# Wide matmuls on high and low parts in two of seven products, and attention's values as a set of products

## The chip, the cores and the metric

The kernel runs on one core of a Trainium2 chip. The metric is device microseconds for one execution, from runs on the chip. A kernel is run several times, and the median is compared.

TensorE (PE in the profile) multiplies: it holds a stationary tile of up to 128x128 numbers, streams a moving tile of up to 512 columns past it, and adds the result to a bank of PSUM, of which there are eight with 512 columns of float32 each. VectorE (DVE), ScalarE (ACT) and GpSimd (POOL) work on tiles in SBUF. SyncE (SP), ACT and POOL also issue DMA transfers. Every engine takes its own instructions in order.

## The reference, cut to what matters

One block on 512 tokens of width 1024, all in float32: a feed-forward stage, a mixer and a second feed-forward stage, each added to x, and a last norm.

```python
def swiglu(x, w_gu, w_down):
    g, u = jnp.split(x @ w_gu, 2, axis=-1)
    return (jax.nn.silu(g) * u) @ w_down

def hybrid_mixer(h, w_in, conv_w, gate_w_up, gate_b, gla_norm_g, w_out_conv, w_out_gla, w_o):
    z = h @ w_in
    cb, cc, cu, q, k, v, g_lr, r, ga, gb = jnp.split(z, SPLIT_POINTS, axis=-1)
    y_conv = (cb * causal_short_conv(cc * cu, conv_w)) @ w_out_conv
    log_a = jax.nn.log_sigmoid((g_lr @ gate_w_up + gate_b).astype(jnp.float32)) / GATE_TAU
    o = gla_chunked(q, k, v, log_a)            # 4 heads, chunks of 64 tokens
    ...                                        # o: norm by head, times gla_norm_g
    y_gla = (o * jax.nn.silu(r)) @ w_out_gla
    merged = jax.nn.sigmoid(ga) * y_conv + jax.nn.sigmoid(gb) * y_gla
    return merged @ w_o

def reference(x, ...):
    x = x + 0.5 * swiglu(rmsnorm(x, norm_ffn1_g), ffn1_w_gu, ffn1_w_down)
    x = x + hybrid_mixer(rmsnorm(x, norm_mix_g), w_in, ...)
    x = x + 0.5 * swiglu(rmsnorm(x, norm_ffn2_g), ffn2_w_gu, ffn2_w_down)
    return rmsnorm(x, final_norm_g)
```

The hidden width of the feed-forward stages is 2816; the mixer's `w_in` has 8208 columns, of which 1024 make attention's values `v`.

## The kernel before, in words

**Numbers in two parts.** TensorE multiplies float32 numbers rounded to a shorter form (`F32R`). Each operand is therefore split: ACT casts it to a high part `h`, DVE subtracts that from the number for a low part `l` (weights: `wh` and `wl`, L309 and L310). A product is three matmuls: high by high, high by low, low by high.

**Sets of seven products.** Most matrices are multiplied two by two blocks at a time with seven products instead of eight, named `m1`, `p2`, `q6`, `p5`, `q7`, `p4`, `p3`. Their operands are sums of blocks. On the weight side, `s3` is a sum by DVE (L296), and three more sums are accumulating DMA transfers of POOL (`f<-f`, L287). On x's side `Operands.sum` makes the sums and `Operands.make` splits them once for all sets of a stage. A set (`Set`, L478) keeps three banks: `a`, `b` and `c`. Each product is 24 matmuls of 256 columns (L501). After `m1`, `q6` and `q7`, ACT copies bank `b` to SBUF (L506), and `done` adds such copies to the banks `a` and `c` with DVE. `order` interleaves neighbouring sets: `m1` of the next one comes ahead of `p4` of this one, then `p2` of the next, `p3` of this, and `q6`, `p5`, `q7` of the next.

**The stages.** A feed-forward stage (`ffn`) makes four plain pairs of gate and up columns (`mm_group`, `mm_single`, 512-column matmuls), then nine sets of two pairs each (`up_set`), then the down product (`down_product`): two sets with 512-column matmuls whose moving operand is the weights (`run_wide`, order of products `SEQ`), and the last six k-tiles plainly. The mixer (`mixer`) makes queries and keys of heads 0 and 1 with `mm_group`, half of `v` with `mm_wide` (L378 to L380), queries and keys of heads 2 and 3 with `mm_single`, the second half of `v`, then twelve sets listed in `MSETS`, the eight columns of `w_out_conv`, two sets of `w_out_gla` (`gla_done`), and `w_o`. Attention's steps for a head (`gates`, `decays`, `scale`, `scores`, `state`, `output`, `squares`) are put between these matmuls by hand, from the dictionary `hooks`. While `normed` overwrites x in place, x itself waits in DRAM (`xs`) and comes back with `reload` (L1453) for the sum in `evac`.

**Weights.** `Weights` works ahead: `take` hands out a split weight tile and has the tiles two steps ahead cast and split; `fetch` asks for plain tiles up to `early` steps ahead, and `phase` plans the loads of a set six steps ahead of its `m1`. Raw tiles share ten buffers (`f`), split ones three each (`wh`, `wl`).

**Order and memory.** The framework takes the instructions in the program's order as priorities and settles each engine's order and each tile's buffer when it builds the program. PSUM has one pool `ps` of six banks (`MM`) for the whole kernel and one of two (`AUX`).

Of the kernel before, what the change touches and what calls it, by code (L numbers as in the profile page):

```python
# [56 lines left out]


def wide(mat, kt, col):
    return [(mat, k0, 2, (col,), 512) for k0 in range(0, kt, 2)]  # L60
# [61 lines left out]
MSETS = [("ga", 0), ("gb", 0), ("conv", 0), ("ga", 1), ("conv", 1), ("gb", 1), ("conv", 2),  # L122
# [7 lines left out]
def wide_sets(mat):  # L130

    for w in range(WIDE):
        subs = []
        for u in range(2):
            subs.append(len(PLAN))
            PLAN.extend((mat, 8 * w + 4 * j + 2 * u, 2, (512 * c,), 512)
                        for c in range(2) for j in range(2))
        for p in SEQ:
            STEPS.extend((n, p) for n in subs)


def ffn_plan(up, down, plain, slow):
# [6 lines left out]
    wide_sets(down)  # L149
# [4 lines left out]
def mixer_plan():  # L154
    units(group("w_in", KD, (QO, KO, QO + P, KO + P)))
    units(wide("w_in", KD, VO))
# [3 lines left out]
    units(wide("w_in", KD, VO + 512))  # L160
# [23 lines left out]
def block_kernel(ctx: ExitStack, tc: tile.TileContext, xT, vecs, gf, gup, wgl, wts, out):  # L184
# [6 lines left out]
    ps = ctx.enter_context(tc.tile_pool(name="ps", bufs=6, space=bass.MemoryType.PSUM))  # L191
# [21 lines left out]
    def MM():  # L213
        cnt[0] += 1
        return ps.tile([P, S], F32, tag="mm", name=f"mm{cnt[0]}")
# [27 lines left out]
    class Weights:  # L243
# [13 lines left out]
        def phase(self, early, first=6):  # L257
# [12 lines left out]
        def fetch(self, at):  # L270

            for n, p in STEPS[at : min(at + self.early, self.end)]:
                if p is None and n not in self.raw:
                    self.raw[n] = self.dma(n)
                elif p is not None and STEPS[at][1] is None:
# [75 lines left out]
    def mm_group(mat, kt, cols, ah, al, extra=None, slow=False):  # L351
        o = [MM() for _ in cols]
        n = len(cols)
        for u in group(mat, kt, cols, slow):
            h, l = W.take(u)
            for i in range(u[2]):
# [6 lines left out]
                if extra is not None:  # L363
                    extra(k)
        return o

    def mm_wide(mat, kt, col, ah, al, extra=None):
        o = [MM() for _ in range(NTB)]
        for u in wide(mat, kt, col):
            h, l = W.take(u)  # L370
            for i in range(u[2]):
                k = u[1] + i
                wh = h[:, i * 512 : (i + 1) * 512]
                wl = l[:, i * 512 : (i + 1) * 512]
                for t in range(NTB):
                    a = ah[k][:, t * P : (t + 1) * P]
                    b = al[k][:, t * P : (t + 1) * P]
                    nc.tensor.matmul(o[t], a, wh, start=k == 0, stop=False)  # L378
                    nc.tensor.matmul(o[t], a, wl, start=False, stop=False)
                    nc.tensor.matmul(o[t], b, wh, start=False, stop=k == kt - 1)  # L380
# [97 lines left out]
    class Set:  # L478
# [8 lines left out]
        def run(self, p):  # L487
# [5 lines left out]
            bh, bl = self.group.get(p)  # L493
# [1038 lines left out]
```

## Time and profile before

| | |
|---|---|
| median of 3 runs | 1191.23 us (1188.14 to 1192.05) |
| the profiled execution | 1192.07 us, its span 1190.4 us |
| mean granted TensorE clock | 0.997 |
| busy share of the span | PE 99%, weight loads 91%, DVE 74%, ACT 53%, POOL 10% |
| matmuls | 7818, of them 5376 with 256 columns in sets |
| DMA | 197.10 MB, 166 GB/s |

The rows of the groups read: line, engine, operation, out<-in by the program's names, stationary and moving shape, count; then busy time in us, mean ns of one; then idle time before them and what ended it. The rows of a timeline and of the chain read: start in us, duration, what. The rows of a window read: its stretch and length, busy us of PE, PEld (weight loads), DVE, ACT and POOL with the counts, then granted clock, the share of the DMA engines and GB/s. The rows of waits read: who waited, for whom, us in total, times, longest.

### The profile page before, as it was taken

What the parts mean: (1) busy time and instruction counts of PE and PEld (TensorE: products, weight loads), DVE (VectorE), ACT (ScalarE), POOL (GpSimd) and SP (SyncE); (2) the same over time, 40 slices, a digit from 0 to 9 for tenths busy, and PEclk for the clock granted to TensorE, in tenths of its full rate; (3) what the DMA queues carried; (4) which work ended last, traced back from release to release, by engine and by line L of the source; (5) the groups of instructions that cost most, each with busy time, mean ns of one, the idle gap of its engine ahead of it and who ended that gap; (6) DMA issues with size and microseconds to landing.
All of it is one profiled execution on the core that took longest, in us unless ns stands there. A gap on an engine that the chain in (4) does not pass through costs nothing. (4 is left out here: it accounts for less than half of the span.)

```text
span 1190.4 us, 19195 instructions
## 1 busy us (share of the span) xinstructions
PE 1177.9 (99%) x7818; PEld 1085.6 (91%) x7818; DVE 878.5 (74%) x1044; ACT 625.5 (53%) x777; POOL 116.3 (10%) x155
## 2 busy tenths in 40 slices
PE   9999999999999999999999999999999999999997
PEld 8899999988788889999999998988889999998876
DVE  7976666897578765868688688676598666679955
ACT  6564454675245465646454566543345454566543
POOL 0011111101010001011111100200001101101100
PEclk9999999999999999999999999999999999999999
DMA  9477777678532325766877766741537777757721
GB/s 349 85 207 187 183 181 191 153 196 209 195 110 85 89 71 149 205 179 178 206 218 176 189 181 200 208 128 54 186 72 210 173 193 176 182 156 192 170 81 71
DMA packets 61224, 197.10 MB, mean 166 GB/s; under 512 B 6768, under 2 KB 13040, under 8 KB 61136
## 3 DMA queue, kind: packets, MB, share of 16 engines
q0 software_dynamic: 18560, 67.12, 30.7%
q1 hardware_dynamic: 37936, 124.27, 29.8%
q10 hardware_dynamic: 4640, 4.49, 1.2%
q8 instruction: 61, 1.00, 0.3%
q14 instruction: 27, 0.22, 0.1%
HBM read 124.55 MB, written 8.39 MB: 112 GB/s over the span
## 5 line engine op out<-in xcount | busy, mean ns | idle before, releaser
L501 PE MATMUL mm<-op,wh 128*128 128x256 f32 x3584 | 649.6, 284 | 2.8 <-ACT tp L506 2.8
L309 ACT CAST wh<-f 128x1024 fp32r<-128x1024 f32 (+1 forms) x335 | 350.1, 1046 | 439.4 <-PE mm L501 227.2
L501 PEld LDWEIGHTS mm<-op,wh 128*128 128x128 f32 x3584 | 560.2, 192 | 4.0 <-ACT tp L506 3.0
L310 DVE TENSOR_TENSOR wl<-f,wh 128x1024 fp32r<-128x1024 f32 (+1 forms) x335 | 406.9, 1217 | 182.2 <-ACT wh L309 176.5
L501 PE MATMUL mm<-op,wl 128*128 128x256 f32 x1792 | 508.1, 284 | 0.1
L501 PEld LDWEIGHTS mm<-op,wl 128*128 128x128 f32 x1792 | 344.0, 192 | 0.6 <-DVE wl L310 0.5
L287 POOL DMA_DIRECT2D f<-f x120 | 103.5, 866 | 922.1 <-DVE wl L310 477.1
L337 PE MATMUL mm<-op,wh 128*128 128x512 f32 x192 | 75.1, 391 | 0.0
L339 PE MATMUL mm<-op,wl 128*128 128x512 f32 x192 | 74.9, 390 | 0.0
L338 PE MATMUL mm<-op,wh 128*128 128x512 f32 x192 | 74.7, 389 | 0.0
L361 PE MATMUL mm<-op,wh 128*128 128x512 f32 x256 | 63.8, 391 | 0.2 <-DVE op L412 0.2
L791 PE MATMUL mm<-wl,op 128*128 128x512 f32 x160 | 62.6, 391 | 0.8 <-DVE wl L310 0.8
L789 PE MATMUL mm<-wh,op 128*128 128x512 f32 x160 | 62.3, 389 | 0.0
L793 PE MATMUL mm<-wh,op 128*128 128x512 f32 x160 | 62.2, 389 | 0.0
L361 PEld LDWEIGHTS mm<-op,wh 128*128 128x128 f32 x256 | 47.8, 188 | 10.6 <-issue 0.4
L506 ACT COPY tp<-mm 128x512 f32<-128x512 f32 x96 | 55.7, 580 | 1.9 <-DVE tp L1299 1.0
L296 DVE TENSOR_TENSOR f<-f,f 128x1024 f32<-128x1024 f32 x40 | 48.8, 1221 | 0.7
L339 PEld LDWEIGHTS mm<-op,wl 128*128 128x128 f32 x192 | 36.0, 188 | 7.5
L337 PEld LDWEIGHTS mm<-op,wh 128*128 128x128 f32 x192 | 36.1, 188 | 7.4
L338 PEld LDWEIGHTS mm<-op,wh 128*128 128x128 f32 x192 | 36.1, 188 | 7.4
L791 PEld LDWEIGHTS mm<-wl,op 128*128 128x128 f32 x160 | 30.0, 188 | 7.8 <-DVE wl L310 1.9
L789 PEld LDWEIGHTS mm<-wh,op 128*128 128x128 f32 x160 | 30.0, 188 | 6.3
(282 smaller groups left out, 1328.8 us busy)
## 6 DMA issues: line engine op xcount, KB each, us to landing
f<-wts SPq DMA_DIRECT2D x219, 512.0 KB, 4.4
f<-f POOLq DMA_DIRECT2D x120, 512.0 KB, 5.0
X<-xT SPq DMA_DIRECT2D x8, 256.0 KB, 5.2
xs<-X POOLq DMA_DIRECT2D x8, 256.0 KB, 2.3
ga<-tp ACTq DMA_DIRECT2D x8, 256.0 KB, 3.0
gb<-tp ACTq DMA_DIRECT2D x8, 256.0 KB, 4.9
tp<-ga SPq DMA_DIRECT2D x8, 256.0 KB, 6.0
X<-xs POOLq DMA_DIRECT2D x8, 256.0 KB, 7.5
```

The costliest lines, as they stand in the source:

```text
L287: nc.gpsimd.dma_start(out_, a, accum_op=ALU.add)
L309: self.cast = nc.scalar.copy(h[:, :w], raw[:, :w]).ins
L310: nc.vector.tensor_tensor(out=l[:, :w], in0=raw[:, :w], in1=h[:, :w].bitcast(F32), op=ALU.subtract)
L337: nc.tensor.matmul(o, wh, ah, start=first, stop=False)
L338: nc.tensor.matmul(o, wh, al, start=False, stop=False)
L339: nc.tensor.matmul(o, wl, ah, start=False, stop=last)
L361: nc.tensor.matmul(o[c], w[:, s : s + P], a[k], start=k == 0 and j == 0, stop=k == kt - 1 and j == 2)
L501: nc.tensor.matmul(to, ww[:, s], aa[:, t], start=fresh and k == 0 and e == 0 and j == 0, stop=k == 3 and j == 2, skip_group_check=True)
L506: nc.scalar.copy(v, o)
L789: nc.tensor.matmul(o[t], bh[:, s], wh, start=fresh and k == 0, stop=False, skip_group_check=True)
L791: nc.tensor.matmul(o[t], bh[:, s], wl, start=False, stop=False, skip_group_check=True)
L793: nc.tensor.matmul(o[t], bl[:, s], wh, start=False, stop=k == 3, skip_group_check=True)
```

## The change

1. **Up sets.** `up_set` uses a new `PairSet`. In products `p5` and `p3`, x's operand lies with its high and low part side by side (`Both`), and the high weights are multiplied by both at once: 8 matmuls of 512 columns, then 8 of 256 for the low weights by the high part. Bank `c` becomes a pair of banks (`MM2`); its halves are added by two DVE operations.
2. **First sums.** In all sets but a stage's first (`forked`), ACT copies the bank of `m1` into a new bank `a`, and `p2` adds to it; DVE's addition of `m1` goes. `q7`'s copy in up sets gets its sign on ACT.
3. **PSUM.** The pool of six banks is opened anew for each stage (`banks`); in the up sets it is two single banks and two pairs, and bank `a` comes from the other two.
4. **Values.** `v` is a set of seven products with 512-column matmuls (`natural_set`, taken from `run_wide`) behind the four single products. Since it is multiplied from the normed x, keys are scaled by the row once instead of by its square. Gates, decays and scaling of head 0 go between the single products, and all later steps of attention move to later sets; two sets of `MSETS` change places.
5. **x.** Each k-tile of x is read back by SP into a tile of its own during `w_out_conv`; POOL's eight reads go.
6. **Weight loads.** Inside sets, `fetch` looks three steps ahead instead of `early`; a set behind wide ones loads eight steps ahead.

```diff
-MSETS = [("ga", 0), ("gb", 0), ("conv", 0), ("ga", 1), ("conv", 1), ("gb", 1), ("conv", 2),
+MSETS = [("ga", 0), ("gb", 0), ("ga", 1), ("conv", 0), ("gb", 1), ("conv", 1), ("conv", 2),
...
 def mixer_plan():
     units(group("w_in", KD, (QO, KO, QO + P, KO + P)))
-    units(wide("w_in", KD, VO))
     for h in (2, 3):
         units(single("w_in", KD, QO + h * P))
         units(single("w_in", KD, KO + h * P))
-    units(wide("w_in", KD, VO + 512))
+    wide_sets("w_in", 1, VO)
...
+    def banks():
+        cnt[0] += 1
+        stack = ExitStack()
+        pools["ps"] = stack.enter_context(tc.tile_pool(
+            name=f"ps{cnt[0]}", bufs=6, space=bass.MemoryType.PSUM, reuse_waits="tile"))
+        return stack
+
+    def MM(bufs=6):
+        cnt[0] += 1
+        return pools["ps"].tile([P, S], F32, tag="mm", name=f"mm{cnt[0]}", bufs=bufs)
+
+    def MM2():
+        cnt[0] += 1
+        return pools["ps"].tile([P, 2, S], F32, tag="mm2", name=f"mm2_{cnt[0]}", bufs=2)
...
                 if p == "m1":
-                    self.loads.setdefault(max(lo, i - first), []).append(n)
+                    after = STEPS[i - 1][1] is not None and PLAN[STEPS[i - 1][0]][4] > HW
+                    wait = PLAN[n][4] == HW and after
+                    self.loads.setdefault(max(lo, i - (8 if wait else first)), []).append(n)
...
-            for n, p in STEPS[at : min(at + self.early, self.end)]:
+            inside = at < self.end and STEPS[at][1] is not None
+            for n, p in STEPS[at : min(at + (3 if inside else self.early), self.end)]:
...
+    class PairSet:
+        DUP = ("p5", "p3")
...
+            if fresh:
+                self.bank[n] = {"a": AUX, "b": lambda: MM(2), "c": MM2}[n]()
...
+            if p in self.DUP:
+                for k in range(4):
+                    for e in range(2):
+                        nc.tensor.matmul(o[:, e], h[:, k * HW + e * P : k * HW + (e + 1) * P],
+                                         x_.both(k), start=fresh and k == 0, stop=False,
+                                         skip_group_check=True)
+                for k in range(4):
+                    for e in range(2):
+                        nc.tensor.matmul(o[:, e, :HW], l[:, k * HW + e * P : k * HW + (e + 1) * P],
+                                         x_.high(k), start=False, stop=k == 3,
+                                         skip_group_check=True)
+            else:
...
+            if p == "m1" and self.forked:
+                self.bank["a"] = AUX()
+                nc.scalar.copy(self.bank["a"], o)
+            elif p in ("m1", "q6", "q7"):
+                v = T()
+                nc.scalar.activation(v, o, AF.Copy, scale=-1.0 if p == "q7" else 1.0)
+                self.v[p] = v
+            self.done(self, p)
...
+        def add(self, n, t, sign=1.0):
+            o = self.bank[n]
+            for c in (HW, 0):
+                part = o[:, :, c : c + HW]
+                nc.vector.scalar_tensor_tensor(
+                    out=t, in0=part, scalar=sign, in1=t, op0=ALU.mult, op1=ALU.add)
...
+    class Both:
+        def __init__(self, v):
+            self.t = []
+            for i in range(2):
+                t = tile_of("op", [P, 2, 2, HW], F32R)
+                w = v[:, 2 * i : 2 * i + 2]
+                nc.scalar.copy(t[:, :, 0], w)
+                nc.vector.tensor_tensor(out=t[:, :, 1], in0=w, in1=t[:, :, 0].bitcast(F32),
+                                        op=ALU.subtract)
+                self.t.append(t)
...
+        def both(self, k):
+            return self.t[k // 2][:, k % 2].rearrange("p a t -> p (a t)")
...
+    def natural_set(ops, banks, done, ahead=1):
+        used = {"a"}
+        for at, p in enumerate(SEQ):
+            for q in SEQ[at : at + ahead + 1]:
+                ops.make(q)
...
+            for u in range(2):
+                h, l = W.take()
+                for i in range(2):
+                    k = 2 * u + i
+                    wh, wl = (a[:, i * 512 : (i + 1) * 512] for a in (h, l))
+                    for t in range(2):
+                        bh, bl = (f(k, t * P, (t + 1) * P) for f in (b_.high, b_.low))
+                        nc.tensor.matmul(o[t], bh, wh, start=fresh and k == 0,
+                                         stop=False, skip_group_check=True)
+                        nc.tensor.matmul(o[t], bh, wl, start=False, stop=False,
+                                         skip_group_check=True)
+                        nc.tensor.matmul(o[t], bl, wh, start=False, stop=k == 3,
+                                         skip_group_check=True)
+            done(p, o)
...
+        stage.close()
+        stage = banks()
         run_sets(up_set)
+        stage.close()
+        stage = banks()
...
-            mul(QK[h][:, 1], o, row2)
+            mul(QK[h][:, 1], o, row)
...
+        steps = [lambda: gates(0), decays, lambda: scale(0)]
+        for h in range(2, HEADS):
+            for c, evac in ((QO, evac_q), (KO, evac_k)):
+                o = mm_single("w_in", KD, c + h * P, xh, xl)
+                if steps:
+                    steps.pop(0)()
+                if c == QO:
+                    xo.make("p2" if h == 3 else "m1")
+                elif h == 2:
+                    xo.sum("p5")
+                evac(h, o)
+        A = [MM(), MM()]
+        natural_set(xo, {"a": A, "b": [MM(), MM()], "c": [MM(), MM()]}, v_done)
...
+        chain = [(0, "q6", state, 0), (0, "q7", output, 0), (0, "p3", squares, 0),
+                 (1, "q6", gates, 1), (1, "q7", None, 1), (1, "p4", scale, 1),
...
+                 (7, "q7", state, 3), (7, "p4", output, 3), (8, "q6", squares, 3)]
...
+        x_old = [QK[2 + i][:, j] for i in range(2) for j in range(2)] + [
+            pools["g"].tile([P, S], F32, tag=t, name=f"{t}_x") for t in ("sc", "reset", "gup_w", "glr")]
...
                 oo.make(AT[d])
+            nc.sync.dma_start(x_old[d], xs[d])
...
-            for k in range(KD):
-                nc.gpsimd.dma_start(x[k], xs[k])
...
-            nc.vector.tensor_tensor(out=x[d], in0=o, in1=x[d], op=ALU.add)
+            nc.vector.tensor_tensor(out=x[d], in0=o, in1=x_old[d], op=ALU.add)
```

More of the change, by code (lines that the diff above doesn't have):

```diff
@@ L1227, in pair @@
+        for n, p, f, h in chain:
+            hooks[n, p] = [(lambda f=f, h=h: f(h)) if f else decays]
+        hooks[2, "p3"] = [pads]
         def pair(t):
@@ L1259, in done @@
                 if p == "p2":
[L1260 to L1261 removed]
+                    s.t1 = s.first()
+                    if s.forked:
+                        s.t1 = T()
+                        nc.scalar.copy(s.t1, bank["a"])
                 if p == "q7":
@@ L1484, in block_kernel @@
         n2 = Norm(V_G2)
-        mixer(nm, n2)
+        with banks():
+            mixer(nm, n2)
     with phase("small3", **FFN):
```

256 lines of the change are left out of this document (122 added, 134 removed).

## The prediction, made before the changed kernel had run

> **What bounds the kernel now.** I read the page's list of engines first, then the groups by line and form, the chain that ended last, the list of waits, and last the timeline at the places that the change touches. TensorE is busy 99% of the span, and the lower line of the clock shows nothing but nines.
>
> ```profile
> span 1190.4 us, 19195 instructions
> PE 1177.9 (99%) x7818; PEld 1085.6 (91%) x7818; DVE 878.5 (74%) x1044; ACT 625.5 (53%) x777; POOL 116.3 (10%) x155
> PEclk9999999999999999999999999999999999999999
> ```
>
> Matmuls overlap, so a busy share says little; the spacing of their starts does. The chain gives it: stretches in which one matmul follows another with nothing between.
>
> ```profile
> 800.79 21.79 PE mm L361 x96
> 1017.66 20.16 PE mm L501 x168
> ```
>
> L501 streams 256 columns and takes 20.16 / 168 = 0.1200 us from start to start; L361 streams 512 and takes 21.79 / 96 = 0.2270 us. Two narrow ones cost 0.2400, one wide 0.2270: 13.0 ns are saved where two become one. The product of a set is 24 narrow ones, 2.88 us, and 224 of them stand in these rows (5376 / 24):
>
> ```profile
> L501 PE MATMUL mm<-op,wh 128*128 128x256 f32 x3584 | 649.6, 284 | 2.8 <-ACT tp L506 2.8
> L501 PE MATMUL mm<-op,wl 128*128 128x256 f32 x1792 | 508.1, 284 | 0.1
> ```
>
> Almost nothing else costs TensorE time. These are the waits of its queue for another engine that are over half a microsecond, without the start:
>
> ```profile
> PEld mm L501 <- ACT tp L506: 3.0, 1, 3.0
> PEld mm L791 <- DVE wl L310: 1.9, 3, 1.2
> PEld aux L791 <- DVE wl L310: 0.9, 1, 0.9
> ```
>
> So the kernel is a row of matmuls with about 6 us of holes. A matmul taken out is worth its spacing, and whatever the change does on DVE, ACT, POOL or the DMA queues counts only where it opens or closes a hole.
>
> **The up products (gain).** In `p5` and `p3` of the two feed-forward stages, 16 narrow matmuls of the high weights become 8 wide ones on the high and low operand side by side; the 8 narrow ones of the low weights stay. New product: 8 x 0.2270 + 8 x 0.1200 = 2.776 us, against 2.88: 0.104 saved. Each stage has 9 sets (11 pairs of columns less 2 plain ones), so 2 x 9 x 2 = 36 products: **-3.7 us**. Could changing the width cost something? The trace switches both ways:
>
> ```profile
> 49.53 0.39 PE L339 MATMUL mm<-op,wl 128*128 128x512 f32 x1
> 49.75 0.40 PE L501 MATMUL mm<-op,wh 128*128 128x256 f32 x2
> ...
> 231.56 0.28 PE L501 MATMUL mm<-op,wl 128*128 128x256 f32 x1
> 231.68 0.40 PE L789 MATMUL mm<-wh,op 128*128 128x512 f32 x1
> ```
>
> Wide to narrow 0.22, narrow to wide 0.12: each takes the spacing of the one that goes first, so a switch is free. Bounds of this term: 0 and 3.7.
>
> The Trainium skill ("TensorE: Matmul & The Clock Gate", section "Wait — 56ns, not 53.3ns?") puts the fixed cost of a warm matmul at about 2.5 ns over its columns, a rule that speaks against this part: by it 36 x 8 matmuls fewer would give, as an estimate, 0.7 us. The rows above disagree with it for this kernel's matmuls.
>
> **The values (gain).** Attention's `v` was two halves of 96 wide matmuls (64 in each of the lines L378 to L380, of which the first is shown); it becomes one set of 7 products with 24 wide matmuls, 168.
>
> ```profile
> L378 PE MATMUL mm<-wh,op 128*128 128x512 f32 x64 | 24.9, 390 | 0.0
> ```
>
> 24 fewer at 0.2270: **-5.4 us**. It adds on DVE two sums `s3`, four evacuations and six more weight splits (14 instead of 8), on POOL six more accumulating DMAs, on ACT two copies more than the eight there were. These lie beside 38 us of matmuls (168 x 0.2270), except at the start of the set, costed below.
>
> **x in plain tiles (gain).** Before, POOL issued eight reads of x while the accumulating DMAs of the `w_out_gla` sets went through the same queue. The chain there:
>
> ```profile
> 759.85 4.31 POOL L1453 DMA_DIRECT2D X<-xs x8 [6.09 <-DVE op L550]
> ...
> 767.07 9.21 DMA f<-f
> ...
> 786.86 4.77 DMA f<-f
> ...
> 792.68 0.59 ACT tp L506
> ...
> f<-wts SPq DMA_DIRECT2D x219, 512.0 KB, 4.4
> f<-f POOLq DMA_DIRECT2D x120, 512.0 KB, 5.0
> ...
> 712.10:755.60 43.50, 43.50 (x195) 36.03 (x194) 34.08 (x36) 27.63 (x35) 3.44 (x4) 1.00 0.63 177
> ```
>
> An accumulation issued at 767.07 takes 9.21 us where the median is 5.0; the 4.2 us run through ACT's cast and DVE into the next one and end as the 3.0 us hole. The eight reads now go to SP's queue, one for each column of `w_out_conv` (the last row: 43.5 us at 177 GB/s, which 8 x 256 KB more bring to about 225), into tiles whose last readers are attention's and gone by then. What is queued behind each on SP is one weight tile or gate, due a column later. **-3.0 us**; bounds 0 (another transfer is late in its place) and 3.0.
>
> **Copies of `m1` into the accumulator (no cost, small margin).** In every set but the first, ACT copies `m1` from bank to bank, and `p2` adds on top, so DVE's addition goes. But `p2` now waits for that copy, with one product between; `q6`, three products on, waited before. The copy is the same length (L797: 570 ns; L506: 580). In a typical set:
>
> ```profile
> 107.72 0.28 PE L501 MATMUL mm<-op,wl 128*128 128x256 f32 x1
> 107.92 1.05 ACT L309 CAST wh<-f 128x1024 fp32r<-128x1024 f32 x1 [1.35 <-PE mm L501]
> 108.88 0.58 ACT L506 COPY tp<-mm 128x512 f32<-128x512 f32 x1
> ...
> 110.72 0.40 PE L501 MATMUL mm<-op,wh 128*128 128x256 f32 x2
> L506 ACT COPY tp<-mm x96: 567/580/596, 54.7 to 1064.8; 128x512 f32<-128x512 f32 x96
> L797 ACT COPY mm<-mm x4: 570/570/570, 236.7 to 1078.7; 128x512 f32<-128x512 f32 x4
> ...
> 49.70:231.60 181.90, 181.77 (x1513) 181.47 (x1513) 130.66 (x132) 95.62 (x115) 23.51 (x28) 1.00 0.73 181
> ```
>
> `m1`'s last matmul starts at 107.72; the copy sits behind one cast and ends at 109.46; `p2` starts at 110.72. Margin 1.26 us, so 0. On DVE an up set loses one operation and gains two (0.69 us each in 20 us; it is 130.66 of 181.90 us busy there), covered likewise.
>
> **Start of the mixer (cost).** The values used to run first, 22 us wide, and hid head 0's gates, decays and scaling; these now lie beside the four single products, 21.8 us, after which `m1` of the values must have its operand. DVE had no room in that stretch:
>
> ```profile
> 371.00:393.40 22.40, 22.40 (x101) 18.49 (x100) 21.27 (x34) 15.21 (x21) 0.00 (x0) 1.00 0.23 71
> L310 DVE TENSOR_TENSOR wl<-f,wh 128x1024 fp32r<-128x1024 f32 x333 | 405.5, 1220 | 177.9 <-ACT wh L309 172.2 <-PE aux L445 4.2 <-DMA f<-wts 0.5
> L1007 DVE SCALAR_TENSOR_TENSOR qk<-mm,row 128x512 f32<-128x512 f32 x2 | 1.4, 688 | 3.8 <-PE mm L339 3.8
> ```
>
> 21.27 of 22.40 us busy. Into it come two `s3` sums, one more split, the sum of `p5` and `p2`'s low part (5 x 1.22, all of the split's size) and three evacuations (3 x 0.69), less the square of the row (0.69): 7.5 us. Of it 1.1 find the idle time and 2.1 the time until the second half of `m1` starts (24.5 us after the group): 4.3 us late. That is the upper bound, if DVE keeps the program's order; the lower is 0, since x's second half and the parts of `p2` and `p5`, over 5 us, are not needed until later products. I take **+2.5 us**.
>
> **PSUM handed over between stages (cost).** One ring of six banks becomes a new division at each stage: two single banks and two pairs in the up sets, six singles elsewhere. So a stage's first matmuls can land on a bank that the last one has just filled. DVE there:
>
> ```profile
> 49.28 0.68 DVE L475 TENSOR_TENSOR tp<-mm,row 128x512 f32<-128x512 f32 x1
> 51.02 0.68 DVE L475 TENSOR_TENSOR tp<-mm,row 128x512 f32<-128x512 f32 x1
> ...
> 232.07 0.68 DVE L705 TENSOR_TENSOR tp<-mm,tp 128x512 f32<-128x512 f32 x1
> ...
> 844.37 0.69 DVE L1459 TENSOR_TENSOR X<-mm,X 128x512 f32<-128x512 f32 x1 [2.05 <-PE mm L339]
> ```
>
> After the last set, `p3`'s two additions end at 232.07 + 2 x 0.68 = 233.4, where the down product wants to start at 231.68: up to 1.75 us, twice; 0 if its first banks were the other pair; I take the middle, 0.75 each. From plain columns to sets, 49.28 + 0.68 is 0.2 past the start at 49.75 (the second read would be 1.95); from `w_out`'s last column to the second stage at most 0.9, of which I take 0.3. Together **+2.0 us**, bounds 0 and 8.
>
> Weight tiles after a set are now asked for three steps ahead, not four or five. A step is 2.7 us or more, and casting starts two steps ahead; a tile's landing (4.4 us median) fits.
>
> ```profile
> 1127.92 5.42 DMA f<-f
> 1133.36 5.74 DMA f<-wts
> 1139.11 1.06 ACT op L309
> ```
>
> The holes at L791 stand at that place, but in the chain the tile's transfer follows an accumulation that held the buffer, not the asking; 0.
>
> **Sum.** -3.7 - 5.4 - 3.0 + 2.5 + 2.0 = -7.6 us. The profiled execution took 1192.07 us (span 1190.4 and 1.7 around it), 0.84 above the median of the runs shown, 1191.23: 1184.5 for an execution like it, **1183.6** for the median. Differences under 0.3%, 3.6 us, a measurement of this kernel can't tell from none: faster means below 1187.7.
>
> **Rivals.**
> *All of it is hidden.* DVE's order favours what is due and the handovers fall on free banks: -12.1, so 1179.1. For it: TensorE waits for DVE in hardly any row now. Against: the 21.27 of 22.40.
> *The costs eat the gain.* DVE's order is the program's (4.3), the handovers cost 5, and x's reads make another transfer late (gain 9.1): 1191.4. Whatever is 4.1 us or more above the forecast's costs falls here, as no difference that can be told; I put its middle at 1189.5.
> *Fewer starts save nothing.* The 13 ns belong to the stream, not to the start: the first term is 0, and 1187.3. Against it, both spacings hold through 96 and 168 matmuls. The skill's 2.5 ns above is nearly this case.
> *Slower: `p2` waits for its copy.* 27 sets (8 and 8 up, 11 in the mixer) have the copy one product ahead. It decides once the copy is later than now by 1.26 us and then (7.6 + 3.6) / 27 = 0.41: one cast more in front of it (1.05) and a copy (0.58) would do, 1.63 against 1.67, then all 27 lose 0.4 and the time is some 1194 to 1195; two casts (2.1) give 0.84 x 27 - 7.6 = +15, or 1206. For it: ACT runs in order, and gates and decays put chains of ACT work beside `m1`. Against: 53% busy, and the one cast in front is there already.
>
> **How the numbers follow.** Forecast with costs of 2 to 8 us, 1181 to 1187: 0.45; all hidden 0.22; costs eat the gain 0.20; starts save nothing 0.04; copies 0.09. Faster is the first, second and fourth, 0.71; same 0.20; slower 0.09. The range goes from 1177.5, the second case less a little, to 1190.5, most of the third; that leaves out under 2 in 10.
>
> **What would show it.** An up set of 168 starts in 20.16 us now has 152 in 19.95; 168 wide matmuls make `v`; no hole at the `w_out_gla` sets; accumulations there near 5 us. In the list of waits, TensorE for DVE's split or `op` at the start of `v` shows the first cost, TensorE for DVE at the first matmul of a down product or of the second stage's group the other. Wrong it would be by a wait of L501-like matmuls for ACT's bank-to-bank copy in set after set, or if the up set kept its 20.16.

## The result, and the profile after

The changed kernel takes 1199.62 us (median of 6 runs, 1197.58 to 1202.47) against 1192.0 for the kernel before beside it (1188.14 to 1192.96): ratio 1.0071, 95% interval 1.0051 to 1.0092. The profiled execution took 1198.0 us, its span 1195.9. The prediction was 1183.6, in a range from 1177.5 to 1190.5.

The page of after, its span, engines and granted clock:

```profile
span 1195.9 us, 18621 instructions
PE 1173.6 (98%) x7506; PEld 1065.2 (89%) x7506; DVE 893.7 (75%) x1067; ACT 634.9 (53%) x794; POOL 116.9 (10%) x153
PEclk9999999999999999999999999999999999999999
```

312 of 7818 matmuls are gone, 8 in each of 36 up products and 24 in the values, and the span is 5.5 us longer. The waits of TensorE's weight loads, us in total, times, longest:

```profile
PEld mm L713 <- DVE wl L319: 6.2, 8, 1.5
PEld mm L491 <- ACT tp L499: 3.7, 2, 3.1
PEld aux L713 <- DVE wl L319: 2.6, 3, 0.9
PEld mm L711 <- ACT wh L318: 2.4, 1, 2.4
PEld aux L1104 <- DVE g L1086: 1.7, 1, 1.7
PEld mm L491 <- ACT mm L496: 1.3, 1, 1.3
PEld mm L370 <- DVE X L1572: 1.0, 1, 1.0
```

Before, the rows over half a microsecond came to 5.8 us, without the wait at the program's start; these come to 18.9, and three more of 0.6 or 0.7 make it 20.8. L711 to L715 are `natural_set`, L491 the narrow `Set`, L1104 the gate's matmuls at the mixer's start, L370 the plain products.

The next table is read from the timelines: us from the first matmul of a stage to the first of the next one, in the profiled executions. The mixer counts from its first gate matmul, which stands 6.6 us behind its first product both before and after; the last row ends with the span. The last two columns are versions explained below.

| stage | before | after | after - before | mended | fork_in_order |
|---|---|---|---|---|---|
| first stage, plain columns | 48.65 | 48.58 | -0.1 | 48.44 | 48.51 |
| first stage, up sets | 181.93 | 180.76 | -1.2 | 181.73 | 181.84 |
| first stage, down product | 118.08 | 123.85 | +5.8 | 118.86 | 117.81 |
| mixer up to its sets | 95.50 | 86.53 | -9.0 | 86.49 | 85.25 |
| mixer's twelve sets | 266.95 | 277.53 | +10.6 | 274.56 | 275.18 |
| `w_out_conv` | 43.55 | 43.55 | 0.0 | 43.55 | 43.55 |
| `w_out_gla` sets | 44.87 | 40.97 | -3.9 | 40.95 | 40.94 |
| `w_o` and second stage's plain columns | 87.56 | 88.46 | +0.9 | 88.43 | 87.56 |
| second stage, up sets | 184.89 | 183.96 | -0.9 | 184.47 | 184.90 |
| second stage, down product | 117.28 | 120.58 | +3.3 | 118.34 | 117.90 |

The hole at the `w_out_gla` sets is closed, the up sets are shorter, and the mixer, read over both rows since attention's steps moved from the one to the other, is 1.6 us longer. The largest losses lie in the down products, whose code the change moved into a function and left alone otherwise.

### The profile page after: what moved, and what is told of

It reads as the page before. It is cut to its first block, busy times and chain, and to the rows that moved or that the text cites. A ratio compares the mean times of both kernels' runs of the same rounds, so it can differ in the third digit from the quotient of the medians.

```text
span 1195.9 us, 18621 instructions
## 1 busy us (share of the span) xinstructions
PE 1173.6 (98%) x7506; PEld 1065.2 (89%) x7506; DVE 893.7 (75%) x1067; ACT 634.9 (53%) x794; POOL 116.9 (10%) x153
## 5 line engine op out<-in xcount | busy, mean ns | idle before, releaser
L318 ACT CAST wh<-f 128x1024 fp32r<-128x1024 f32 (+1 forms) x341 | 356.0, 1046 | 393.1 <-PE mm L491 91.0
L319 DVE TENSOR_TENSOR wl<-f,wh 128x1024 fp32r<-128x1024 f32 (+1 forms) x341 | 413.5, 1217 | 181.4 <-ACT wh L318 170.7
L491 PE MATMUL mm<-op,wh 128*128 128x256 f32 x1568 | 285.2, 284 | 4.4 <-ACT tp L499 3.3
L491 PEld LDWEIGHTS mm<-op,wh 128*128 128x128 f32 x1568 | 245.0, 192 | 6.0 <-ACT tp L499 3.7
L491 PE MATMUL mm<-op,wl 128*128 128x256 f32 x784 | 222.8, 284 | 0.3 <-DVE wl L319 0.2
L547 PE MATMUL mm<-op,wh 128*128 128x256 f32 x1152 | 210.2, 284 | 0.3 <-ACT wh L318 0.3
L547 PEld LDWEIGHTS mm<-op,wh 128*128 128x128 f32 x1152 | 179.7, 192 | 1.0 <-ACT wh L318 0.5
L547 PE MATMUL mm<-op,wl 128*128 128x256 f32 x576 | 162.9, 283 | 0.0
L491 PEld LDWEIGHTS mm<-op,wl 128*128 128x128 f32 x784 | 150.2, 192 | 0.8 <-DVE wl L319 0.7
L547 PEld LDWEIGHTS mm<-op,wl 128*128 128x128 f32 x576 | 110.4, 192 | 0.0
L713 PE MATMUL mm<-wl,op 128*128 128x512 f32 x216 | 85.7, 397 | 3.4 <-DVE wl L319 3.4
L711 PE MATMUL mm<-wh,op 128*128 128x512 f32 x216 | 84.6, 393 | 2.0 <-ACT wh L318 2.0
L715 PE MATMUL mm<-wh,op 128*128 128x512 f32 x216 | 84.8, 393 | 0.0
L346 PE MATMUL mm<-op,wh 128*128 128x512 f32 x192 | 74.7, 389 | 0.0
L347 PE MATMUL mm<-op,wh 128*128 128x512 f32 x192 | 74.7, 389 | 0.0
L533 PE MATMUL mm<-op,wh 128*128 128x512 f32 x288 | 72.6, 393 | 0.3 <-ACT wh L318 0.3
L370 PE MATMUL mm<-op,wh 128*128 128x512 f32 x256 | 64.1, 392 | 1.0 <-DVE X L1572 0.6
L533 PEld LDWEIGHTS mm<-op,wh 128*128 128x128 f32 x288 | 51.7, 189 | 9.7 <-ACT wh L318 0.6
L370 PEld LDWEIGHTS mm<-op,wh 128*128 128x128 f32 x256 | 47.7, 188 | 11.7 <-DVE X L1572 1.0
L572 DVE SCALAR_TENSOR_TENSOR tp<-mm,tp 128x512 f32<-128x512 f32 x72 | 49.4, 686 | 9.3 <-PE mm L538 8.8
```

The source lines that it names most:

```text
L318: self.cast = nc.scalar.copy(h[:, :w], raw[:, :w]).ins
L319: nc.vector.tensor_tensor(out=l[:, :w], in0=raw[:, :w], in1=h[:, :w].bitcast(F32), op=ALU.subtract)
L346: nc.tensor.matmul(o, wh, ah, start=first, stop=False)
L347: nc.tensor.matmul(o, wh, al, start=False, stop=False)
L370: nc.tensor.matmul(o[c], w[:, s : s + P], a[k], start=k == 0 and j == 0, stop=k == kt - 1 and j == 2)
L491: nc.tensor.matmul(to, ww[:, s], aa(k), start=fresh and k == 0 and e == 0 and j == 0, stop=k == 3 and j == 2, skip_group_check=True)
```

## The experiments

Two bases were used: the changed kernel with single parts undone, and the kernel before with single parts added (first x in plain tiles, `x_alone`, then more). "Ratio" is to the kernel before on the same chip.

**1. Parts undone and x alone.**

```diff
# x_alone: before, with x read back in plain tiles
-                nc.gpsimd.dma_start(x[k], xs[k])
+            nc.sync.dma_start(x_old[d], xs[d])
# narrow_up: after, every up product narrow; narrow_last: the last set's alone
-            if p in self.DUP:
+            if p in self.DUP and not self.narrow:
# no_fork: after
-            sets[n].forked = i > 0
+            sets[n].forked = False
```

> The kernel before with x read back in plain tiles and nothing else of the change. Theory (the gains of the prediction came, and new holes at the borders of stages ate them): the 3.0 us hole at the w_out_gla sets closes and nothing else moves, 1192.0 - 3.0 = 1189 us. Rival (another transfer is late in place of the accumulation): 1192.

> The changed kernel with narrow matmuls in all products of the up sets; bank c is then a single bank and its addition one DVE operation instead of two. Theory: 18 sets lose their 0.17 us each (+3.1), and the holes behind the up sets, 3.5 us and a lowered clock of 1.7 us in the first stage and about 3.5 us in the second, close: 1199.6 + 3.1 - 7.5 = about 1195 us. Rival (the holes come from the copies of m1 or from the shorter look-ahead of the weight loads): the holes stay, 1202.7.

> The changed kernel with narrow matmuls and a single bank c in the last up set of each stage alone. Theory: the two-step addition after the last p3, with the in-order ACT queue behind it, opens the holes at the down products: 0.35 us of the gain is lost, 7 us of holes close, 1199.6 + 0.35 - 7 = about 1193 us. Rival (DVE is late from the additional operations of all the sets, or by something else): 1199.9.

> The changed kernel with m1 copied to SBUF and added by DVE in every set, as before. Theory: only the 1.3 us hole in the mixer, where p2 waits for its copy behind gates and decays, goes: about 1198 us. Rival (the copies into the accumulator, one product ahead of p2 on an in-order ACT, make most of the new 15 us of holes): 1191 or less.

Measured: `x_alone` 1188.57 us, ratio 0.9988 (0.9978 to 0.9998), with the `w_out_gla` sets at 41.86 for 44.87; a hole of 1.3 us stays there. `narrow_up` 1201.85 (1.0104; 1.0088 to 1.0121): its up sets are 2.1 and 1.8 us longer than in after, but the down products stay long, 121.9 and 121.8. `narrow_last` 1200.18 (1.0084; 1.0068 to 1.0100): first down product 118.75, second 123.2. `no_fork` 1198.41 (1.0078; 1.0055 to 1.0101), with 120.9 and 121.1: the time expected, but by luck. The mixer's sets, where the 1.3 us hole was to go, are 1.0 us longer than in after; the first down product is 3.0 us shorter. So the theory fell in its first form: undoing any one part cures one down product at most, and more than the addition after the last `p3` had to be at work.

These runs can be read fully only with POOL's order, which part 4 finds. In `narrow_up` at both down products, and in `narrow_last` at the second, two accumulating transfers stand in another order than before, and ACT waits for the landing of the later one. POOL and ACT in `narrow_last`:

```profile
1074.49 1.77 POOL L296 DMA_DIRECT2D f<-f  x2 [5.99 <-DMA f<-f]
1082.02 1.04 ACT L318 CAST wh<-f 128x1024 fp32r<-128x1024 f32 x1 [3.83 <-DMA f<-f]
```

In `narrow_last` at the first down product, which came out at 118.75, the order is that of before.

**2. Parts added one at a time to `x_alone`.**

```diff
# x_fetch: plain weight tiles inside sets three steps ahead
+            for n, p in STEPS[at : min(at + (3 if inside else self.early), self.end)]:
# x_banks: the pool of six banks opened anew for each stage
+        stage.close()
+        stage = banks()
# x_pair: x_banks with PairSet, without copies into the accumulator
+            return PairSet(xo, done)        # forked = False
# x_values: natural_set for v with its hooks; Set, one pool, forked = False
```

> The kernel before with x in plain tiles, and plain weight tiles inside sets asked for three steps ahead. The profile of the change has 5.8 and 3.3 us more in the two down products. Theory A (the shorter look-ahead makes the weights of the down products late): 1188.6 + 6 to 9 = 1195 to 1198 us, with both down products 3 us longer or more. Theory B (the division of PSUM by stage does it) and theory C (the orders of DVE and ACT, settled anew for every kernel, do it): within 1 us of 1188.6.

> The kernel before with x in plain tiles, and the pool of six banks opened anew for each stage, six single banks in each. Theory B (a down product's first banks come from the stage before, and its work on DVE starts late): 1188.6 + 6 to 9 = 1195 to 1198 us, in the down products. Theories A and C: within 1.5 us of 1188.6, with 0.7 us between w_o and the second stage, as in the changed kernel.

> The kernel before with x in plain tiles, stage by stage banks, and the wide matmuls in p5 and p3 of the up sets with their pair of banks, without the copies into the accumulator, the values' set and the shorter look-ahead. The gain alone: 1188.6 - 3.7 = 1184.9 us. Theory B: the down products lose 6 to 9, 1191 to 1194. Theory C (DVE has one operation more in each set and orders its work anew): up sets 1 us shorter each, down products 1 to 4 us longer each, 1188 to 1194.

> The kernel before with x in plain tiles and the values as a set of products, with attention's steps moved as in the change; narrow up sets, one pool of banks, no copies into the accumulator, the old look-ahead. By the prediction's terms 1188.6 - 5.4 + 2.5 = 1185.7 us. Theory (the raw buffers are all held by the values' set, the first mixer set's loads and accumulations come late, the 3.0 us hole stands behind it; nothing waits at its start): the mixer's sets begin with a hole of 3 us, 1188.6 - 5.4 + 3 to 4.5 = 1186 to 1188.

Measured: `x_fetch` 1189.12 (0.9981; 0.9969 to 0.9993), down products 118.0 and 117.2: theory A falls. `x_banks` 1195.42 (1.0043; 1.0029 to 1.0056): 6 us, though not where theory B had them: 1.3 at the mixer's start, 3.1 at the second stage's start, 1.2 in the second down product. Three of its waits:

```profile
PEld mm L806 <- ACT wh L320: 2.7, 3, 1.2
PEld aux L1016 <- DVE g L998: 1.7, 1, 1.7
PEld aux L754 <- ACT X L755: 1.3, 1, 1.3
```

The second is the same 1.7 us at the mixer's first gate matmul as in after. `x_pair` 1199.77 (1.0074; 1.0054 to 1.0094): up sets 181.7 and 184.4, down products 121.1 and 123.4, a time above all that was expected. The wide matmuls with their pair of banks cost in the next stage four times what they save in their own. `x_values` 1191.72 (1.0016; 1.0007 to 1.0026): the mixer's sets begin with the expected hole, but the time is 4 us above the expected range.

**3. DVE's additions, loads and borders.**

```diff
# two_adds: x_banks, a second operation that adds zero times the bank
+                    nc.vector.scalar_tensor_tensor(out=g2, in0=bank["c"], scalar=0.0, in1=g2,
+                                                   op0=ALU.mult, op1=ALU.add)
# one_add: x_pair, the second half left out
-            for c in (HW, 0):
+            for c in (0,):
# later_loads: x_values
-                    first = 6
+                    first = 3 if wait else 6
# two_borders: x_banks, pool reopened before and behind the up sets only
-        with banks():
-            mixer(nm, n2)
+        mixer(nm, n2)
```

> x_banks (narrow matmuls everywhere) with bank c's additions after q7 and p3 of the up sets done in two DVE operations each, the second adding zero times the bank. Theory D (two more DVE operations of 0.69 us in an up set make DVE late where the down product begins): the down products become 3 and 5 us longer than in x_banks, as with the wide matmuls: 1200 to 1203 us. Rival (the pair of banks, the operand's new layout or the wide matmuls themselves delay the down product): 1195.4 to 1197.

> x_pair with one of the two additions left out after q7 and p3 (the second half of the pair of banks, the product with x's low part, isn't added). Theory D: the up sets keep their 1.0 and 0.8 us, the down products return to the length that they have in x_banks: x_pair's 1199.8 - 3.1 - 5.0 = 1191 to 1193 us. Rival: the down products stay long, 1198 to 1200.

> x_values with the loads of the second mixer set three steps later, so that they do not share the DMA engines with the first set's accumulations. Theory (the first accumulation takes 7.6 us beside these loads, the next one comes late, and the hole of 2.5 us with the lowered clock behind it, 4.2 us in all, follows): the hole goes, 1191.7 - 4.2 = 1187.5 us. Rival (only the raw buffers' release counts, and the loads of the second set are late then): 1191 to 1193.

> x_banks with the pool opened anew only before and behind each stage's up sets, and kept from the first down product through the mixer to the second stage's plain columns. Theory B for the rest (at each reopening the first matmuls wait for the last evacuations of the stage before, or stand in another order): the 1.3 us at the mixer's start and the 3.1 us at the second stage's start go, 1195.4 - 4.4 = 1191 us. Rival (the division inside the feed-forward stages does it): 1194 to 1195.

Measured: `two_adds` 1201.67 (1.0094; 1.0058 to 1.0130), the time that theory D gave, but at another place and so by luck: the down products have x_banks' length (118.1 and 118.9), and the loss stands ahead of their first matmul, twice 3.4 us. For the weight load there the profile names no cause, but for the matmul it does:

```profile
PE mm L810 <- DVE tp L720: 6.8, 2, 3.4
```

L720 is the second addition out of bank `c` after the last `p3`; DVE does it at 234.14, behind a weight split, and the first matmul of the down product starts at 234.97, when it has ended. This is a handover of a PSUM bank between stages, the cost that the prediction put at 0.75 us. In `x_banks` the first matmul of each down product stands 1.05 us, until the one addition (L717, to 232.73) and a cast of ACT (to 232.83) have ended; in after it doesn't stand at all.

`one_add` 1196.73 (1.0053; 1.0035 to 1.0072): 120.6 and 120.8, so 0.5 and 2.6 of the 3.1 and 5.0 us are gone, and the rest is not the second addition. `later_loads` 1191.98 (1.0006; 0.9993 to 1.0019): no gain, and it told nothing about the loads, since the requests to SP stood at the same times as in x_values, within 0.5 us; it seems that they go out when a buffer is free, whatever step asks. `two_borders` 1193.13 (1.0021; 1.0009 to 1.0034): the mixer's start is back at 95.5, the second stage's start keeps 2.2 of its 3.1 us; neither theory gave this time.

**4. The causes in the trace.** Behind the values' set, ACT in `x_values` stood for an accumulation that POOL had issued 7 us before. POOL, ACT, then windows behind the hole (granted clock third from last):

```profile
432.51 1.76 POOL L292 DMA_DIRECT2D f<-f  x2 [8.65 <-DVE f L301]
440.60 1.99 ACT L314 CAST wh<-f 128x1024 fp32r<-128x1024 f32 x2 [4.93 <-DMA f<-f]
443.30:446.50 3.20, 3.20 (x16) 3.20 (x16) 2.47 (x3) 0.72 (x1) 0.00 (x0) 0.50 1.01 202
```

The cast is that of `q6`'s weight, two products behind `m1` in the first set; there the steps are 2.7 us long, where half of `v` came in steps of 5.4 us before. At the down products, one of the in-place sums of the down product's own operand moved behind the border in `x_pair` (border at 232.2). It has one at 222.8 and then these two; `wide_six`, explained below, has two at 221 and 223 and the third behind the border, as the kernel before has:

```profile
238.43 1.22 DVE L687 SCALAR_TENSOR_TENSOR hidw<-hidw 128x1024 f32<-128x1024 f32 x1
240.70 1.22 DVE L687 SCALAR_TENSOR_TENSOR hidw<-hidw 128x1024 f32<-128x1024 f32 x1
```

And DVE had no time to give there even before. The kernel before, windows of 20 us from the border on (third busy time is DVE's):

```profile
232.00:252.00 20.00, 20.00 (x90) 16.55 (x89) 19.86 (x20) 17.75 (x22) 2.77 (x4) 1.00 0.71 157
252.00:272.00 20.00, 20.00 (x90) 16.57 (x89) 19.97 (x20) 12.52 (x14) 2.58 (x3) 1.00 0.83 228
```

```diff
# p5_first: x_values, order of the first set in the mixer
-        seq += [(s, "q6"), (s, "p5"), (s, "q7")]
+        mid = ("p5", "q6", "q7") if late and i == 0 else ("q6", "p5", "q7")
+        seq += [(s, p) for p in mid]
# p5_first_fork: the same, forked in the up sets
# less_dve: after, four of seven subtractions left out in each first down set
+            if rough:
+                self.l = self.h
+                return
# wide_six: x_pair, up sets 7 to 9 narrow with one addition
+            s.narrow = i > 5
```

> x_values with p5 ahead of q6 in the mixer's first set. Theory E: behind the values' set, whose steps are half as long as those before, q6's weight has two steps less from m1's split to its own cast, and its accumulation (7.1 us beside another one) lands 2.5 us late; one product more in between covers that, and the lowered clock behind the hole goes with it: 1191.7 - 2.5 - 1.7 = 1187.5 us, under the kernel before. Rival (the raw buffers, all held by the values' set, make the whole first set late): the hole moves to p5 or q6 and stays over 1.5 us, 1190 to 1192.

> p5_first with ACT's copy of m1 into a new bank in the up sets, so that DVE has one operation of 0.69 us less in each. Theory D (DVE is full from the end of the up sets through the first 40 us of the down product, and any DVE time saved or added there shows on TensorE): the 1.2 us holes of the down products shrink, 0.5 to 1.5 us less than p5_first, 1186 to 1187 us. Rival (ACT's copy ahead of p2 costs as much): the same as p5_first or 1 us more.

> The changed kernel with four of the seven low-part subtractions of x's side left out in the first set of each down product (the high part is used again in their place): 4 x 1.22 = 4.9 us less DVE at each of the two borders, and nothing else. Theory D: the holes there are DVE's backlog, so 4 of the 5.8 us in the first and 3 of the 3.3 in the second down product go: 1199.6 - 7 = 1192 to 1194 us. Rival (the borders wait for banks, weights or the ACT queue): 1198 to 1200.

> x_pair with the wide matmuls and two additions in the first six up sets of each stage, and narrow ones with one addition in the last three. Theory D (what counts is DVE's work at the border, and the sets long before it have room): the down products as long as in x_banks (118.0 and 118.4 us), the up sets keep two thirds of the gain: 1195.4 - 1.2 - 2.2 (the second stage's start) = 1191 to 1193 us. Rival (the pool's division by pairs or the operand's layout costs the down products): they stay at 121 and 123 us, 1199.

Measured: `p5_first` 1187.77 (0.9976; 0.9965 to 0.9988): theory E holds; the hole is gone and the sets are 3.9 us shorter than in x_values. `wide_six` 1192.58 (1.0014; 1.0004 to 1.0025): down products 118.75 and 119.5; most of the cost came from the sets next to the border. `less_dve` 1196.62 (1.0042; 1.0026 to 1.0058): 2.2 and 2.4 us less in the down products, less than theory D asked for. At the first one POOL's order (next) differs from after's too, so that decides nothing; at the second it is after's, so the 2.4 us speak for theory D, though 1.0 of them returns ahead of the product. `p5_first_fork` 1196.39 (1.0044; 1.0030 to 1.0058) went against theory D: one DVE operation less in each up set, and the down products 5.1 and 3.6 us longer. Its POOL and ACT at the first one show why:

```profile
231.91 1.75 POOL L293 DMA_DIRECT2D f<-f  x2 [4.31 <-DMA f<-f]
240.55 1.04 ACT L315 CAST wh<-f 128x1024 fp32r<-128x1024 f32 x1 [5.03 <-DMA f<-f]
```

A down set's matmuls come in two halves, each with its own accumulations. Without the copies POOL issues `a21 += a22` of the second half as soon as DVE's sum `s3` is there. In the kernel before:

```profile
229.57 0.86 POOL L287 DMA_DIRECT2D f<-f  x1 [2.60 <-DVE f L296]
231.33 0.86 POOL L287 DMA_DIRECT2D f<-f  x1 [0.89 <-DVE hid L700]
```

With the copies, the build puts `a11 += a21` of the first half ahead of it. That one has to wait for the landing of the first half's `a21 += a22` (the 4.31), the second half's follows in the same row, and `p5`'s second weight waits for it. After has the same row at its first down product, and behind it ACT's cast for L711, the 2.4 us in the list of waits:

```profile
230.99 1.75 POOL L296 DMA_DIRECT2D f<-f  x2 [4.17 <-DMA f<-f]
237.77 1.99 ACT L627 CAST op<-hidw 128x1024 fp32r<-128x1024 f32 x2 [2.24 <-DVE hidw L673]
239.67 1.04 ACT L318 CAST wh<-f 128x1024 fp32r<-128x1024 f32 x1
243.00:247.00 4.00, 4.00 (x12) 3.14 (x11) 3.97 (x4) 3.74 (x6) 0.00 (x0) 0.57 0.48 116
```

But here ACT doesn't stand for the landing. The later accumulation was issued at 231.5 and landed 7.4 us on, at 238.9; ACT was then in two casts of the product's other operand, which had waited for two of DVE's in-place sums in a row, and went on to L711's weight without a pause. `no_fork` has the same two holes of TensorE, 2.0 and 1.1 us, at its second down product, with POOL's order that of before:

```profile
1082.07 1.99 ACT L627 CAST op<-hidw 128x1024 fp32r<-128x1024 f32 x2 [2.23 <-DVE hidw L673]
1083.97 1.04 ACT L318 CAST wh<-f 128x1024 fp32r<-128x1024 f32 x1
```

So two late chains end within 0.8 us of each other in the changed kernel's first down product, DVE's sums with ACT's casts last and POOL's accumulation just ahead.

**5. The order put back.**

```diff
# fork_in_order: p5_first_fork; mended: after with this, p5 first and narrow = i > 5
+                self.last_sum = self.add(a21, a22)
...
+            if p == "m1" and PLAN[n][4] > HW:
+                with tc.issue_after(self.last_sum):
+                    self.add(a11, a21)
```

> p5_first_fork with one edge of order more: in the sets with 512-column matmuls POOL issues the accumulation a11 += a21 of the first half behind the accumulation a21 += a22 of the second half, as it stands in the versions without the copies. Theory F (with the copies POOL's order has these two swapped, p5's second weight lands 5 us late, and ACT and DVE behind it with it): the down products return from 123.1 and 122.5 us to 118 and 118.9, 1196.4 - 8.5 = 1188 us. Rival (ACT's copies themselves delay the border): no change, 1196.

> The changed kernel with three edits, each of which acts in a stage of its own: the wide matmuls only in the first six up sets (narrow in the last three), the same edge of order on POOL, and p5 ahead of q6 in the mixer's first set. Theories D, E and F together: first down product 123.9 to 118.8, second 120.6 to 119.5, the mixer's sets 277.5 to 274, the up sets 0.6 longer each: 1199.6 - 5.1 - 1.1 - 3.7 + 1.2 = 1191 us, which leaves the costs of the reopened pool. Rivals: any stage that keeps its length keeps its own other cause.

Measured: `fork_in_order` 1187.41 (0.9976; 0.9966 to 0.9986), down products 117.8 and 117.9; POOL and ACT again:

```profile
229.89 0.86 POOL L293 DMA_DIRECT2D f<-f  x1 [3.14 <-DVE f L302]
230.99 0.86 POOL L293 DMA_DIRECT2D f<-f  x1 [0.23 <-issue]
238.54 1.05 ACT L315 CAST wh<-f 128x1024 fp32r<-128x1024 f32 x1
```

ACT's 5 us wait is gone: theory F holds, and the copies themselves cost nothing there. With p5_first this is the best version, 0.24% below the kernel before, though not told apart from p5_first. `mended` 1190.25 (0.9993; 0.9983 to 1.0003): the three stages come out near what was expected (118.9, 118.3, 274.6), 9 us below the changed kernel and level with the kernel before. In the first down product two of the three edits act together, but the runs above that start from the changed kernel undo them one by one. Lengths of the first down product:

| last up sets | accumulations swapped | in the order of before |
|---|---|---|
| wide | after 123.85 | `no_fork` 120.85 |
| narrow | `narrow_up` 121.91 | `narrow_last` 118.75, `mended` 118.86 |

Read down, the wide last sets cost 1.9 to 2.1 us there; read across, the order costs 3.0 to 3.2, and both together undone give nearly the 118.08 of before. The order in these columns is more than POOL's: in `no_fork` DVE's two sums no longer stand together either, and how much of the 3.0 us is which stays open. After and `narrow_up` also have 3.4 us at a clock of 0.50 there, the others none.

## Why the prediction was wrong, step by step

**Up products, -3.7: right in kind, a little large, and not all of it arrives.** Behind the first set, an up set of the first stage takes 19.99 us for 20.16 (19.95 was forecast): 0.17 for 16 matmuls fewer, 10.6 ns each for the 13.0 of the forecast, 3.1 us in 18 sets. The Trainium skill's 2.5 ns for a start ("TensorE: Matmul & The Clock Gate", section "Wait — 56ns, not 53.3ns?"), 0.7 us by the prediction's estimate, does not fit. Against the kernel before the up sets gain 2.1 in all, since a wait of 0.5 to 0.6 us for ACT's cast stands in the first set of each stage. The 3.9 us against `narrow_up` are too much, for that run has a hole of 1.4 us of its own in its first set.

**"On DVE an up set loses one operation and gains two ... covered likewise": failed.** The average of 130.66 in 181.90 us hid the border: from there DVE is busy 19.86 and 19.97 of 20 us, and a sum that used to be done by then moves behind it. `x_pair` against `wide_six`, both with POOL's order of before, prices it at 2.3 and 3.9 us; in the 3.9 is a stretch of 6.8 us at a granted clock of 0.50, which `no_fork` behind the same two holes doesn't have, and its product is 2.3 us shorter. That the cost comes from the last three sets is shown; which part is the additions and which the new order of DVE's instructions stays open (in `one_add` most of it stays without the second addition).

**Copies of `m1`, "no cost, small margin": failed, at another place than the one weighed.** The margin of `p2` held in all sets but one, the 1.3 us of L491 behind ACT's L496, with decays ahead of the copy. What costs is the order that the build settles anew: two accumulations swapped on POOL, 5.3 and 4.6 us in `p5_first_fork` against `fork_in_order`. In the changed kernel the swap stands in the first stage alone. Undoing the copies (`no_fork`) makes the first down product 3.0 us shorter, with the swap gone and DVE's order changed as well; the rest of the kernel loses about as much again, so the time hardly moves. The slower rival named a part that did cost, and the measured time lies between its two (1194 to 1195, and 1206), but that is luck: its mechanism hardly occurred.

**Values, -5.4, "these lie beside 38 us of matmuls, except at the start": failed at the end.** The start, costed at +2.5, has no hole: the term was 0. Behind the set stands the 3.0 us hole, and in `x_values` the lowered clock. Without the hole, in `p5_first`, the mixer gains 1.9 us over `x_alone` (360.3 against 362.2), not 5.4: attention's steps, moved in between the sets, and in the longest wait the convolution's now stand ahead of DVE's weight splits there. In `p5_first` these waits are

```profile
PEld mm L488 <- DVE wl L316: 3.2, 6, 0.9
```

**PSUM handed over, +2.0 of 0 to 8: mis-sized.** `x_banks` costs 6.1 us of span against `x_alone`. The handover from `w_o`, taken at 0.3, is 0.7; those to the down products, taken at 0.75 each, are 1.05 each in `x_banks` and 0 in after. Much of the rest is no handover but order: the gate's first matmul stands four matmuls earlier in TensorE's order than before, ahead of its weights from DVE (1.7 us, in after as well), and in x_banks transposes wait at the second stage's start (1.3 us).

**x, -3.0, and the look-ahead, 0: right in size.** The stage loses 3.0 us in `x_alone`; of it 1.3 show in the medians. But the hole itself only shrinks, from 2.9 to 1.3 us, in `x_alone`. The rest is a lowered clock behind the hole before, 0.50 from 793.3 to 796.6, which the prediction didn't count and which `x_alone` doesn't have. In after the hole is gone.

## What to carry to other kernels

Price a change of the order of work at the borders of stages, in 20 us windows there, not by the share of a stage: an engine at 72% over a stage can be full for the 40 us that follow it. Where a build settles the order of in-order engines anew, compare the order of every queue before and after, the DMA-issuing one too; accumulations swapped in two places cost more in `p5_first_fork` (9.9 us) than 312 matmuls were forecast to be worth (9.1). That holds for experiments as well: undoing one part settles the orders anew, and `narrow_up` seemed to clear the wide matmuls only because the swap on POOL now stood at both of its down products. When the steps ahead of a place become shorter, a look-ahead counted in steps becomes shorter in time.

## What the hardware showed that was not expected

The granted clock falls behind some holes of TensorE and not behind others. In `x_values` a hole of 2.5 us is followed by 3.2 us at 0.50 (window above); in after, holes of 2.1 and 1.4 us close together by 4 us at 0.57; but behind after's longest hole, 3.0 us at 446.5, the clock stays full. In `two_adds` the same hole of 3.4 us occurs twice, and only behind the second does the clock fall. After, then `two_adds`:

```profile
446.50:449.50 3.00, 0.24 (x3) 0.04 (x1) 1.32 (x2) 2.40 (x4) 0.86 (x1) 1.00 0.22 44
449.50:452.60 3.10, 2.97 (x24) 2.97 (x25) 2.77 (x3) 1.03 (x2) 0.00 (x0) 1.00 0.96 198
231.30:235.00 3.70, 0.31 (x4) 0.14 (x2) 3.70 (x6) 2.13 (x3) 1.14 (x2) 1.00 1.03 195
235.00:240.00 5.00, 5.00 (x22) 4.17 (x23) 5.00 (x6) 3.44 (x4) 0.34 (x1) 1.00 1.00 211
1076.00:1079.50 3.50, 0.11 (x2) 0.06 (x1) 3.50 (x5) 2.13 (x3) 1.38 (x2) 1.00 1.02 192
1079.60:1083.00 3.40, 3.40 (x9) 2.66 (x10) 3.40 (x4) 2.28 (x3) 0.25 (x1) 0.50 1.02 190
```

So the length of a hole doesn't decide it alone. The shortest single hole here with a lowered clock behind it is 1.8 us (`x_fetch`, at 790.2); in `narrow_up` two holes of 1.0 and 0.8 us close together had one behind them too. Apart from the programs' ends, a lowered stretch lasts 3.4 us in these runs, in two of them 6.8.

The Trainium skill ("TensorE: Matmul & The Clock Gate", section "What's actually happening") has the clock halve after an idle window of about 3.4 us that runs freely. The half clock fits, the 3.4 us fit the lowered stretches, and a chance of phase fits; that a hole of 1.8 us can be enough does not. The lowered clock makes x_values' hole cost 4.2 us instead of 2.5, by half of 3.4.
